# One transformer block on one core: the attention scan takes two keys per step, and GpSimd fills in the products in between and writes the causal mask

## The chip, the core and the metric

The kernel runs on one core of one Trainium2 chip, as one launch. The metric is the device time of that launch in microseconds. The engines that matter here are TensorE (PE in the profile, with its weight loads as PEld), VectorE (DVE), ScalarE (ACT) and GpSimd (POOL); SP is the engine whose queue issues most of the DMAs. Each engine works through its own list of instructions in order, and waits on the others through semaphores.

## The reference

The program is one layer of a block with 1024 tokens, width 1024 and 16 heads of 64. The part that the change touches is stick-breaking attention: no softmax, but a product over the keys between a key and its query.

```python
for i in range(s_len // Q_BLOCK):              # 8 blocks of 128 queries
    n_keys = i * Q_BLOCK + Q_BLOCK             # only the causal prefix of keys
    z = einsum('bhqd,bhkd->bhqk', qb, kp) / sqrt(dh)
    mask = s_idx < t_idx                       # strictly causal
    log_not = where(mask, log_sigmoid(-z), 0.0)
    excl = cumsum(log_not, reverse=True) - log_not
    log_a = log_sigmoid(z) + excl              # A[t,s] = sigmoid(z_ts) * prod_{s<j<t} (1 - sigmoid(z_tj))
    a = where(mask, exp(log_a), 0.0)
    out_i = einsum('bhqk,bhkd->bhqd', a, vp)
```

Around it stand an input projection to eight sections, a short gated convolution as a second branch, two branch projections, a merge by gates, an output projection, and a gated feed-forward layer. All of it is in float32; the kernel splits each float32 matrix into a high and a low part and multiplies them in three passes.

## The kernel before

The kernel works through stages: the start (norm and first projections), the gates and sections with a Strassen scheme, then attention woven together with projections that do not depend on it, then the merge, the output projection and the feed-forward layer. The change lies in the attention stage alone.

There attention is computed as products, not as sums of logarithms. For one head and one block of 128 queries (128 such steps in all, `h` from 0 to 15, `i` from 0 to 7) the tile `pt` of 128 rows of queries by 1024 columns holds 1 - sigmoid(z) for the `(i + 1) * 128` keys of the prefix, at its right end. A running product from the last key to the first turns it into the shares of the stick that are left; the weight of a key is the difference of two neighbouring shares, and that difference is moved onto the values instead (`att_dv`: the tiles `va` and `vb` are the values of neighbouring keys, and their difference is what the weights are multiplied with). So after the scan `pt` goes straight into the product with the values.

A step has these parts, each on its own engine:

- `att_scores`: PE multiplies a block of queries with the keys into `z`, in pieces of at most 512 keys, first the 512 old keys and then the rest (lines 913 and 914, for the high and the low part of the keys). ACT turns each piece into 1 - sigmoid in `pt` (line 915). Blocks 0 to 3 have one piece, blocks 4 to 7 two. `z` has two PSUM buffers.
- `att_scan`: DVE runs the product over all `(i + 1) * 128` columns, from right to left (line 923). Its second operand is `mk`, a constant tile that is 1 where the mask excludes a key and 0 elsewhere; the scan multiplies and then takes the maximum with `mk`, so that excluded keys leave the product at 1.
- `att_trans`: PE transposes `pt` in blocks of 128 columns into PSUM tiles `tr`, four to a tile (line 936). ACT copies a `tr` to the high part `ath` (line 939), DVE subtracts to get the low part `atl` (line 940). `tr` has three buffers.
- `att_av`: for each pair of query blocks PE multiplies the transposed weights with the values (lines 951 and 952) into `o`; ACT and DVE add the last row and put the two halves together (lines 956 and 958), and SP stores the result.

`attention()` is a generator that sets the order: in step `s` come the scores of `s`, the transposes of step `s - 2`, the scan of `s`, and the product with the values of `s - 3`. `pt` has five buffers. After every piece the loop at the end of the stage puts in some of the filler work (`fillers`: two projections with operands that lie ready, lines 1012 to 1014, in groups of three matmuls of 512 columns), in proportion to the attention work done. After that, a loop chains all PE instructions of the stage, and the DVE instructions that attention itself made, in exactly the order in which the program made them; the rest is ordered by the scheduler of the framework. So on PE the distance between the scores of a step and its transposes is fixed: one full step and a bit of filler.

GpSimd has no work in the stage. Its list goes from the weight sums of the gates (line 747) to the first DMA of the stage after attention (line 1127).

Of the kernel before, what the change touches and what calls it, by code (L numbers as in the profile page):

```python
# [12 lines left out]
ALU = mybir.AluOpType  # L13
# [4 lines left out]
P = 128  # L18
T = 1024
D = 1024  # L20
# [10 lines left out]
def block_kernel(tc, x, x_t, cols, ada_1, ada_2, ada_row, w_q, w_kv, w_cg, w_a, w_b, w_o, w_g, w_u, w_d, out):  # L31
    nc = tc.nc
# [7 lines left out]
    def nm(s):  # L40
        uid[0] += 1
        return f"{s}_{uid[0]}"
# [12 lines left out]
    def load_w(src):  # L55
# [32 lines left out]
    mk = const.tile([P, D], F32, name="mk")  # L88
    nc.gpsimd.memset(mk, 0.0)
    nc.gpsimd.affine_select(out=mk[:, D - P:], in_=mk[:, D - P:], compare_op=ALU.is_ge, fill=1.0, base=-1,  # L90
                            pattern=[[-1, P]], channel_multiplier=1)
# [43 lines left out]
    def tt(eng, out, a, b, op):  # L135
        eng.tensor_tensor(out=out, in0=a, in1=b, op=op)  # L136
# [761 lines left out]
    def att_scores(h, i):  # L898

        sqt, skh, skl = hd[h]
        n = (i + 1) * P
        off = D - n
        npt[0] += 1
        pt = pts[npt[0] % NPT]
        ptof[h, i] = pt
        for s0 in range(0, n, 512):  # L910
            m = min(512, n - s0)
            z = pps.tile([P, 512], F32, tag="z", bufs=NZ, name=nm("z"))
            nc.tensor.matmul(z[:, :m], sqt[:, i * P:(i + 1) * P], skh[:, s0:s0 + m], start=True, stop=False)
            lastz[0] = nc.tensor.matmul(z[:, :m], sqt[:, i * P:(i + 1) * P], skl[:, s0:s0 + m], start=False, stop=True)  # L914
            nc.scalar.activation(pt[:, off + s0:off + s0 + m], z[:, :m], AF.Sigmoid, scale=rq[:, 1, i, h:h + 1])  # L915
            if s0 + m < n:
                yield F_Z
        yield F_Z + F_S * ((i - 1) % 8 + 1)

    def att_scan(h, i):  # L920
        pt, off = ptof[h, i], D - (i + 1) * P
        rev = slice(D - 1, off - 1 if off else None, -1)
        nc.vector.tensor_tensor_scan(out=pt[:, rev], data0=pt[:, rev], data1=mk[:, rev], initial=1.0,  # L923
                                     op0=ALU.mult, op1=ALU.max)

    def att_trans(h, i):
        pt, off = ptof.pop((h, i)), D - (i + 1) * P
# [39 lines left out]
    def attention():  # L967

        steps = [(h, i) for h in range(H) for i in (LAST if h == H - 1 else ORDER)]
        for s in range(len(steps) + DAV):  # L970
            flush[0] = s >= len(steps)
            if s < len(steps):
                h, i = steps[s]
                if s % 8 == (0 if h else 3) and h + 1 < H:
                    with tc.issue_after(lastld[0].ins):
                        att_load(h + 1)
                with tc.issue_after(lastz[0].ins) if s else ExitStack():
                    if s in (1, 2):
                        att_dv(0, s - 1)
                    if s % 8 in ((4, 6) if h % 2 else (3, 5)) and h + 1 < H:  # L980
                        att_dv(h + 1, s % 8 // 5)
                    if s % 16 in (6, 7) and s + 16 < len(steps):
                        load_v(2 * (s // 16) + 2, 7 - s % 16)
                if s == 54:
                    with tc.issue_after(lastld[0].ins):
                        vl = load_vlast(1)
                if s == 56:
                    turn_vlast(1, vl)
                yield from att_scores(h, i)
            tr_ = att_trans(*steps[s - 2]) if 0 <= s - 2 < len(steps) else iter(())  # L990
            av_ = att_av(steps[s - DAV][0], steps[s - DAV][1] // 2) if s >= DAV and s % 2 != DAV % 2 else iter(())
            yield from itertools.islice(tr_, 1)
            if s >= DAV and steps[s - DAV][1] == 5:
                yield from av_
            yield from tr_
            if s < len(steps):
                att_scan(*steps[s])
            yield from av_
# [96 lines left out]
    pe, mine = len(nc.cur_bb.bb.instructions), set()  # L1095
# [13 lines left out]
            pass  # L1109
    prev = {}  # L1110
    for i in nc.cur_bb.bb.instructions[pe:]:
        if i.engine == nc.tensor.engine or i.name in mine and i.engine in (nc.vector.engine,):
            if i.engine in prev:
                tc.add_manual_dep(i, prev[i.engine].name, mybir.DependencyInfo(mybir.DependencyClass.NoSync, mybir.DependencyReason.DATA),
                                  reason="in_order")
            prev[i.engine] = i
# [187 lines left out]
    for ch in range(2):  # L1304
# [21 lines left out]
        for i in (0, 4, 1, 2, 3, 5, 6, 7) if ch else range(8):  # L1326
            n, t0 = i // 4, (i % 4) * P
# [114 lines left out]
    def load_any(src):  # L1442
        nld[0] += 1
        if nld[0] % 4 != 1:
            return load_raw(src)
        raw = cp.tile([P, 1024], F32, tag="rawx", bufs=1, name=nm("raw"))
        nc.sync.dma_start(raw, src)
        return raw

    def s2_tile():  # L1450
        return cp.tile([P, 512], F32, tag="s2", bufs=1, name=nm("s2"))

    first = [load_any(w_g[1]), s2_tile(), load_any(w_g[1 + NJ])]
# [309 lines left out]
```

## Time and profile before

| | |
|---|---|
| median of 3 runs | 1811.62 us (1808.80 to 1814.61) |
| the profiled execution | 1812.88 us, of which its span, from the first to the last instruction, is 1811.1 us |
| granted TensorE clock | 0.998 |
| PE busy | 1786.0 us, 99% of the span |
| DVE busy | 1334.5 us, 74% |
| ACT busy | 825.2 us, 46% |
| POOL busy | 202.2 us, 11% |
| scans of attention, line 923 | 128, 172.3 us of DVE in sum, from 598.7 to 969.9 us |

The profile is one execution. Its page gives busy times for each engine, and groups of instructions by source line and tile with their mean duration and the idle time of the engine just ahead of them. A timeline row gives the start and the length in microseconds, the engine, the line, the operation, output and inputs, their shape, and in brackets the idle time of the engine before it with what ended it. Idle time on an engine other than PE costs nothing by itself, since PE is busy nearly all the time; what counts is idle time of PE.

### The profile page before, as it was taken

To read this page: it belongs to the slowest core of one execution; us is meant where nothing else is said; L and a number is where in the kernel's file an instruction comes from. 1 tells how busy PE (TensorE), PEld (TensorE's weight loads), DVE (VectorE), ACT (ScalarE), POOL (GpSimd) and SP (SyncE) were. 2 spreads that over 40 slices of the span, in tenths; PEclk is the share of its full clock that TensorE was granted. 3 is DMA by queue.
4 is the path that set the end of the run, shared out by engine and by line. 5 is a ranking of instruction groups with operands and counts; after the bars stand their busy time and mean duration, and the time that the engine had idled before them with its cause. 6 is when DMAs were issued, how large, how long until landed. Compare 5 with 4: busy or idle time off the path is not lost.

```text
span 1811.1 us, 24342 instructions
## 1 busy us (share of the span) xinstructions
PE 1786.0 (99%) x8599; PEld 1485.4 (82%) x8599; DVE 1334.5 (74%) x2030; ACT 825.2 (46%) x1553; POOL 202.2 (11%) x181
## 2 busy tenths in 40 slices
PE   8999999999999999999999999999999999999999
PEld 6888877888888788888887878888888888878887
DVE  6876586787774799999996764698867777644776
ACT  5534364233433567666675221674544444422321
POOL 0024243723231000000000100100000000000000
PEclk9999999999999999999999999999999999999999
DMA  9479654223545977796645866324533444389876
GB/s 383 162 238 392 231 175 140 87 99 115 211 130 175 266 186 195 214 311 180 159 126 175 278 212 214 129 104 157 217 129 144 147 186 162 130 300 338 279 230 223
DMA packets 165006, 359.04 MB, mean 198 GB/s; under 512 B 15539, under 2 KB 60939, under 8 KB 163733
## 3 DMA queue, kind: packets, MB, share of 16 engines
q1 hardware_dynamic: 128300, 289.65, 48.9%
q10 hardware_dynamic: 33096, 55.25, 8.5%
q0 software_dynamic: 3488, 12.59, 2.1%
q8 instruction: 68, 1.11, 0.3%
q14 instruction: 54, 0.43, 0.1%
HBM read 247.84 MB, written 109.62 MB: 197 GB/s over the span
## 4 chain that ended last, share of the span: by engine, by line
PE 84%; DVE 6%; DMA 6%; ACT 3%; issue 2%; SPq 0%; ACTq 0%; POOL 0%; DVEq 0%
PE pj L293 9%; PE e L133 7%; PE e L131 7%; PE e L132 7%; PE pj L133 7%; PE pj L131 7%; PE pj L132 7%; PE e L1590 4%; PE e L1591 4%; PE e L1592 4%; PE tr L936 3%; PE pj L1012 2%; PE pj L1013 2%; PE pj L1014 2%; PE o L952 2%
## 5 line engine op out<-in xcount | busy, mean ns | idle before, releaser
L923 DVE TENSOR_TENSOR_SCAN pt<-pt,mk 128x128 f32<-128x128 f32 (+7 forms) x128 | 172.3, 1346 | 1.5 <-ACT pt L915 1.5
L1221 ACT ACTIVATE whi<-raw 128x512 fp32r<-128x512 f32 x137 | 84.9, 628 | 159.5 <-PE e L132 100.0
L1222 DVE TENSOR_TENSOR wlo<-raw,whi 128x512 fp32r<-128x512 f32 x137 | 93.0, 686 | 68.3 <-ACT whi L1221 50.7
L293 PE MATMUL pj<-whi,big 128*128 128x512 f32 x448 | 133.8, 396 | 3.5 <-ACT big L262 3.5
L132 PE MATMUL e<-big,whi 128*128 128x512 f32 x352 | 136.9, 389 | 0.0
L133 PE MATMUL e<-big,wlo 128*128 128x512 f32 x352 | 136.3, 389 | 0.5 <-DVE wlo L1222 0.5
L131 PE MATMUL e<-big,whi 128*128 128x512 f32 x352 | 136.5, 390 | 0.0
L136 DVE TENSOR_TENSOR c<-pj,c 128x512 f32<-128x512 f32 x140 | 93.2, 681 | 45.1 <-PE pj L133 44.8
L131 PE MATMUL pj<-big,whi 128*128 128x512 f32 x320 | 125.0, 391 | 0.0
L133 PE MATMUL pj<-big,wlo 128*128 128x512 f32 x320 | 124.8, 390 | 0.0
L132 PE MATMUL pj<-big,whi 128*128 128x512 f32 x320 | 124.6, 389 | 0.0
L1590 PE MATMUL e<-whi,f 128*128 128x512 f32 (+1 forms) x319 | 121.7, 382 | 2.5 <-DMA f<-d_f 2.5
L1591 PE MATMUL e<-wlo,f 128*128 128x512 f32 (+1 forms) x319 | 121.8, 382 | 0.0
L1592 PE MATMUL e<-whi,f 128*128 128x512 f32 (+1 forms) x319 | 121.6, 382 | 0.0
L915 ACT ACTIVATE pt<-z,rq 128x512 f32<-128x512 f32 (+1 forms) x192 | 105.2, 576 | 23.6 <-PE z L914 23.2
L1012 PE MATMUL pj<-big,whi 128*128 128x512 f32 x256 | 113.6, 444 | 0.0
L940 DVE TENSOR_TENSOR atl<-tr,ath 128x512 fp32r<-128x512 f32 (+1 forms) x192 | 102.8, 549 | 9.5 <-ACT ath L939 7.6
L939 ACT ACTIVATE ath<-tr 128x512 fp32r<-128x512 f32 (+1 forms) x192 | 93.0, 488 | 29.2 <-PE tr L936 28.2
L131 PE MATMUL e<-rh,whi 128*128 128x512 f32 x264 | 102.8, 389 | 1.4 <-DVE c L136 1.4
L293 PEld LDWEIGHTS pj<-whi,big 128*128 128x128 f32 x448 | 84.9, 190 | 22.0 <-ACT big L262 4.3
L132 PE MATMUL e<-rl,whi 128*128 128x512 f32 x264 | 102.7, 389 | 0.0
L133 PE MATMUL e<-rh,wlo 128*128 128x512 f32 x264 | 102.0, 389 | 0.0
(298 smaller groups left out, 4571.5 us busy)
## 6 DMA issues: line engine op xcount, KB each, us to landing
f<-d_f SPq DMA_DIRECT2D x77, 512.0 KB, 4.6
d_f<-fs SPq DMA_DIRECT2D x70, 512.0 KB, 3.2
raw<-w_cg SPq DMA_DIRECT2D x40, 512.0 KB, 3.8
raw<-w_u SPq DMA_DIRECT2D x26, 512.0 KB, 4.2
raw<-w_g SPq DMA_DIRECT2D x25, 512.0 KB, 4.1
raw<-w_kv SPq DMA_DIRECT2D x20, 512.0 KB, 5.1
ld<-ada SPq DMA_DIRECT2D x16, 512.0 KB, 6.9
d_t<-ts SPq DMA_DIRECT2D x16, 512.0 KB, 6.6
```

What stands on the lines that cost most here:

```text
L131: nc.tensor.matmul(ps, wh[:, k, :], fh[:, k, :], start=(k == 0 and not onto), stop=False, skip_group_check=onto)
L132: nc.tensor.matmul(ps, wh[:, k, :], fl[:, k, :], start=False, stop=False, skip_group_check=onto)
L133: nc.tensor.matmul(ps, wl[:, k, :], fh[:, k, :], start=False, stop=(k == 3), skip_group_check=onto)
L136: eng.tensor_tensor(out=out, in0=a, in1=b, op=op)
L293: nc.tensor.matmul(ps, a, b, start=(k == 0 and q == 0), stop=(k == KT - 1 and q == 2))
L915: nc.scalar.activation(pt[:, off + s0:off + s0 + m], z[:, :m], AF.Sigmoid, scale=rq[:, 1, i, h:h + 1])
L923: nc.vector.tensor_tensor_scan(out=pt[:, rev], data0=pt[:, rev], data1=mk[:, rev], initial=1.0, op0=ALU.mult, op1=ALU.max)
L940: nc.vector.tensor_tensor(out=tl[:, :nb, c0:c0 + P], in0=src, in1=th[:, :nb, c0:c0 + P].bitcast(F32), op=ALU.subtract)
L1012: nc.tensor.matmul(ps, wh, rh_, start=(k == 0), stop=False)
L1590: nc.tensor.matmul(o, sh, w[0][:, c], start=(j == 0), stop=False)
L1591: nc.tensor.matmul(o, sh, w[1][:, c], start=False, stop=False)
L1592: nc.tensor.matmul(o, sl, w[0][:, c], start=False, stop=(j == NJ - 1))
```

## The change

Three edits, all in attention.

First, the scan takes two keys per step. `first` is every second column of `pt` from the last one down, `both` the columns in between. The scan multiplies its state with an element of `first` and then with the one of `both`, and writes the product into `both`; it has half as many elements and steps by two columns (8 bytes) backwards. The columns of `first` now lack their value: GpSimd multiplies each with the finished product to its right (`mid`, one instruction per step with `(i + 1) * 64 - 1` elements per row, also in steps of 8 bytes). The transposes of a step wait for that product.

Second, the mask. With two multiplications the scan has no place for the maximum, so GpSimd writes 1 into the excluded places of the last 128 columns before the scan (`affine_select`, one per step of 128 by 128). So that these columns are ready early, the pieces of the scores are made in reverse: for blocks 4 to 7 first the piece with the diagonal, of 128 to 512 keys, then the 512 old keys.

Third, the GpSimd instructions that attention makes are chained in the order of the program, as those of DVE are.

```diff
-        for s0 in range(0, n, 512):
+        for s0 in reversed(range(0, n, 512)):
             m = min(512, n - s0)
...
             nc.scalar.activation(pt[:, off + s0:off + s0 + m], z[:, :m], AF.Sigmoid, scale=rq[:, 1, i, h:h + 1])
-            if s0 + m < n:
+            if s0 + m == n:
+                diag = pt[:, D - P:]
+                nc.gpsimd.affine_select(out=diag, in_=diag, compare_op=ALU.is_ge, fill=1.0, base=-1,
+                                        pattern=[[-1, P]], channel_multiplier=1)
+            if s0:
                 yield F_Z
...
     def att_scan(h, i):
         pt, off = ptof[h, i], D - (i + 1) * P
-        rev = slice(D - 1, off - 1 if off else None, -1)
-        nc.vector.tensor_tensor_scan(out=pt[:, rev], data0=pt[:, rev], data1=mk[:, rev], initial=1.0,
-                                     op0=ALU.mult, op1=ALU.max)
+        first = pt[:, slice(D - 1, off, -2)]
+        both = pt[:, slice(D - 2, off - 1 if off else None, -2)]
+        nc.vector.tensor_tensor_scan(out=both, data0=first, data1=both, initial=1.0, op0=ALU.mult, op1=ALU.mult)
+        mid = pt[:, slice(off + 1, D - 2, 2)]
+        tt(nc.gpsimd, mid, mid, pt[:, slice(off + 2, D - 1, 2)], ALU.mult)
...
-        if i.engine == nc.tensor.engine or i.name in mine and i.engine in (nc.vector.engine,):
+        if i.engine == nc.tensor.engine or i.name in mine and i.engine in (nc.vector.engine, nc.gpsimd.engine):
```

The lists of the engines change as follows. On GpSimd, between the weight sums of the gates and the DMAs of the stage after attention, there is nothing before; now 256 rows stand there, two for each step. Before:

```order
L136 TENSOR_TENSOR ws_4977<-raw_4836 128x512
L136 TENSOR_TENSOR ws_4978<-raw_4836,ws_4979 128x512
L747 TENSOR_TENSOR ws_4980<-raw_4834,ws_4978 128x512
L1127 DMA cab_10045<-ada_row 128x1024
L636 DMA ad_10092<-ada 128x1024
```

Now, at the end of the tenth head (blocks 6 and 7) and the start of the eleventh (line 918 is the mask, line 136 the product in between):

```order
L918 AFFINE_SELECT pt_5113<-pt_5113 128x128
L136 TENSOR_TENSOR pt_5113<-pt_5113 128x447
L918 AFFINE_SELECT pt_5109<-pt_5109 128x128
L136 TENSOR_TENSOR pt_5109<-pt_5109 128x511
L918 AFFINE_SELECT pt_5110<-pt_5110 128x128
L136 TENSOR_TENSOR pt_5110<-pt_5110 128x63
```

So the mask of a step stands behind the product of the step before it, which waits for that step's scan. In the same place DVE has these rows before (a scan is printed as SCALAR_TENSOR_TENSOR; `wlo` is the low part of a filler's weights, `mb` a filler's result, `oy` the result of a pair of blocks):

```order
L923 SCALAR_TENSOR_TENSOR pt_5113<-pt_5113,mk 128x896
L958 TENSOR_TENSOR oy_8036<-o_8026,otmp_8035 64x256
L1062 TENSOR_TENSOR mb_8062<-pj_7929,sgi_7927 128x512
L940 TENSOR_TENSOR atl_8008<-tr_8052,ath_8007 128x4x128
L136 TENSOR_TENSOR wlo_8238<-raw_8231,whi_8237 128x512
L940 TENSOR_TENSOR atl_8020<-tr_8065,ath_8019 128x2x128
L923 SCALAR_TENSOR_TENSOR pt_5109<-pt_5109,mk 128x1024
```

and these now:

```order
L928 SCALAR_TENSOR_TENSOR pt_5113<-pt_5113 128x448
L964 TENSOR_TENSOR oy_8352<-o_8342,otmp_8351 64x256
L1068 TENSOR_TENSOR mb_8381<-pj_8232,sgi_8230 128x512
L946 TENSOR_TENSOR atl_8323<-tr_8371,ath_8322 128x4x128
L136 TENSOR_TENSOR wlo_8577<-raw_8570,whi_8576 128x512
L946 TENSOR_TENSOR atl_8335<-tr_8384,ath_8334 128x2x128
L928 SCALAR_TENSOR_TENSOR pt_5109<-pt_5109 128x512
```

The order is the same; each scan has half the elements and no `mk`. On PE only the two pieces of a block's scores change places. Block 5 of one head before:

```order
L913 MATMUL z_6777<-skh_6305,sqt_6304 128x512
L914 MATMUL z_6777<-skl_6306,sqt_6304 128x512
L1012 MATMUL pj_6740<-big_144,whi_6393 128x512
L1013 MATMUL pj_6740<-big_146,whi_6393 128x512
L1014 MATMUL pj_6740<-big_144,wlo_6394 128x512
L913 MATMUL z_6784<-skh_6305,sqt_6304 128x256
L914 MATMUL z_6784<-skl_6306,sqt_6304 128x256
L936 MATMUL tr_6788<-dm,pt_5113 128x128 x4
```

and now:

```order
L913 MATMUL z_6957<-skh_6433,sqt_6432 128x256
L914 MATMUL z_6957<-skl_6434,sqt_6432 128x256
L1018 MATMUL pj_6915<-big_144,whi_6528 128x512
L1019 MATMUL pj_6915<-big_146,whi_6528 128x512
L1020 MATMUL pj_6915<-big_144,wlo_6529 128x512
L913 MATMUL z_6967<-skh_6433,sqt_6432 128x512
L914 MATMUL z_6967<-skl_6434,sqt_6432 128x512
L942 MATMUL tr_6971<-dm,pt_5113 128x128 x4
```

The PE list has the same rows otherwise, and the lists of ACT and SP differ from before only by rows that changed places with a neighbour or two.

## The prediction

> **What bounds the kernel now.** I read the page's busy times first, then the busy times of the attention stage (600 to 985 us), then who makes PE wait there.
>
> ```profile
> PE 1786.0 (99%) x8599; PEld 1485.4 (82%) x8599; DVE 1334.5 (74%) x2030; ACT 825.2 (46%) x1553; POOL 202.2 (11%) x181
> 600.00:985.00 385.00, 377.71 (x2309) 325.66 (x2307) 353.69 (x497) 256.64 (x581) 2.35 (x4) 1.00 0.72 200
> PE tr L936 <- DVE pt L923: 4.3, 9, 1.8
> PE o L951 <- ACT ath L939: 1.1, 1, 1.1
> PE o L952 <- DVE atl L940: 0.7, 3, 0.3
> PE tr L936 <- DVE atl L940: 0.4, 1, 0.4
> PE z L913 <- ACT pt L915: 0.3, 1, 0.3
> ```
>
> The second row is the stage: its length, then the busy time of PE, PEld, DVE, ACT, POOL. PE is the bound of the kernel and of the stage: 377.71 of 385 us. DVE comes close, 353.69 us or 92%, and has to answer in its fixed order. POOL is empty. The whole prize is what PE idles here: 385 - 377.71 = 7.3 us of 1811. The wait rows (total, times, longest) say that the scan is the main cause, nine times.
>
> The idle column understates a wait. Ends of matmuls are modelled, so starts are the better measure:
>
> ```profile
> 828.46 0.28 PE L914 MATMUL z<-skl,sqt 128*128 128x128 f32 x1
> 828.57 0.63 PE L936 MATMUL tr<-dm,pt 128*128 128x128 f32 x4
> 832.28 0.28 PE L914 MATMUL z<-skl,sqt 128*128 128x256 f32 x1
> 832.77 0.63 PE L936 MATMUL tr<-dm,pt 128*128 128x128 f32 x4 [0.21 <-DVE pt L923]
> ```
>
> Undisturbed, the transposes start 0.11 us behind the last score matmul; with the wait it is 0.49. The row calls it 0.21, PE lost 0.38. So I add 0.17 us to each wait.
>
> Two waits are not DVE's fault and stay. The longest one on the scan is at the start of the stage, where DVE itself waits for a DMA:
>
> ```profile
> 601.83 0.69 DVE L136 TENSOR_TENSOR vb<-vb,va 128x512 f32<-128x512 f32 x1 [2.60 <-DMA vb<-d_v]
> 602.44 0.68 DVE L923 TENSOR_TENSOR_SCAN pt<-pt,mk 128x256 f32<-128x256 f32 x1
> 603.18 0.44 PE L936 MATMUL tr<-dm,pt 128*128 128x128 f32 x2 [1.80 <-DVE pt L923]
> ACT whi L516 <- DMA raw<-w_cg: 3.1, 1, 3.1
> ```
>
> The other is the 1.1 us on `ath`: ACT had stood 3.1 us before a filler weight's DMA. **Removable** is then 7.3 - 1.8 - 1.1 = 4.4 us, plus 0.17 for each of the 13 other waits of the list, 2.2 us: 6.6 us.
>
> **The change part by part.** *The scan* loses half its elements, 128 times.
>
> ```profile
> L923 DVE TENSOR_TENSOR_SCAN pt<-pt,mk 128x128 f32<-128x128 f32 (+7 forms) x128 | 172.3, 1346 | 1.5 <-ACT pt L915 1.5
> L923 DVE TENSOR_TENSOR_SCAN pt<-pt,mk 128x1024 f32<-128x1024 f32 x16 | 36.5, 2279 | 0.0
> L923 DVE TENSOR_TENSOR_SCAN pt<-pt,mk 128x128 f32<-128x128 f32 x16 | 6.6, 414 | 1.5 <-ACT pt L915 1.5
> ```
>
> Between 128 and 1024 elements a scan costs (2279 - 414) / 896 = 2.08 ns per element, on a fixed 0.148 us. With 64 to 512 elements a head's eight scans take 8 x 0.148 + 2304 x 2.08 ns = 5.98 us, all 16 heads 95.6 us, so DVE gains 76.7 us. No row shows a scan in steps of 8 bytes. The bounds are this price and, with a step of two at half the speed, the old 172.3 us. I take the first: the scan already runs backwards at 2 ns per element, so one element has time for two words.
>
> *The product in between*, and *the mask*, are new on POOL. Rows for POOL:
>
> ```profile
> L136 POOL TENSOR_TENSOR ws<-raw,raw 128x512 f32<-128x512 f32 x20 | 29.0, 1452 | 222.1 <-DMA raw<-w_cg 130.5 <-DMA raw<-w_q 29.9 <-DVE cab L136 17.9
> L123 POOL TENSOR_TENSOR rs_r<-rs_m,nhalf 128x8 f32<-128x8 f32 x16 | 28.8, 1800 | 1.2
> L123 POOL TENSOR_TENSOR rs_r<-rs_m,nhalf 128x1 f32<-128x1 f32 x8 | 4.4, 556 | 0.7
> L90 POOL TENSOR_SCALAR_AFFINE_SELECT mk<-mk 128x128 f32<-128x128 f32 x1 | 0.3, 290 | 0.0
> ```
>
> The mask is the same instruction as on line 90: 128 x 0.29 = 37 us. The two small rows are powers, whose elements are dear (1800 - 556) / 7 = 178 ns, but they give the fixed part: 556 - 178 = 0.378 us. The 512-element row then gives (1452 - 378) / 512 = 2.10 ns per element. A head's products have 63 to 511 elements, 2296 in sum: 8 x 0.378 + 2296 x 2.10 ns = 7.85 us, all heads 126 us. POOL is then busy 163 of the stage's 385 us. These rows are contiguous; for steps of 8 bytes the bounds are 2.10 and 4.2 ns (half speed). I take 2.10, the row it is nearest to.
>
> [...]
>
> *The new chain.* A step's transposes now wait for sigmoid, mask, scan and product, and the next step's mask stands behind that product, so steps form a loop over two engines. A handover between them is short: POOL starts 0.09 us behind DVE in the first pair of rows, DVE 0.03 us behind POOL in the second.
>
> ```profile
> 150.10 0.67 DVE L454 TENSOR_REDUCE qss<-qsq 128x8 f32<-128x512 f32 x1
> 150.86 0.20 POOL L122 TENSOR_SCALAR rs_m<-qss 128x8 f32<-128x8 f32 x1 [4.94 <-DVE qss L454]
> 161.91 1.64 POOL L123 TENSOR_TENSOR rs_r<-rs_m,nhalf 128x8 f32<-128x8 f32 x1
> 163.58 0.69 DVE L457 TENSOR_TENSOR qn<-pj,rs_r 128x512 f32<-128x512 f32 x1 [0.79 <-POOL rs_r L123]
> L923 DVE TENSOR_TENSOR_SCAN pt<-pt,mk x128: 411/1346/2281, 598.7 to 969.9; 128x128 f32<-128x128 f32 x16, 128x256 f32<-128x256 f32 x16, 128x384 f32<-128x384 f32 x16, 128x512 f32<-128x512 f32 x16
> ```
>
> Per head the loop is 5.98 + 7.85 + 2.32 + 24 x 0.1 = 18.6 us, while a head has (969.9 - 598.7) / 16 = 23.2 us. It does not bind on average. The tight place is a head's end, where short steps follow the longest scan. I replay it at 828 us:
>
> ```profile
> 825.71 2.01 DVE L923 TENSOR_TENSOR_SCAN pt<-pt,mk 128x896 f32<-128x896 f32 x1
> 828.00 0.38 ACT L939 ACTIVATE ath<-tr 128x256 fp32r<-128x256 f32 x1
> 829.42 0.68 DVE L136 TENSOR_TENSOR wlo<-raw,whi 128x512 fp32r<-128x512 f32 x1
> 830.01 0.42 DVE L940 TENSOR_TENSOR atl<-tr,ath 128x256 fp32r<-128x256 f32 x1
> 830.35 2.28 DVE L923 TENSOR_TENSOR_SCAN pt<-pt,mk 128x1024 f32<-128x1024 f32 x1
> ```
>
> Before, the long scan starts at 830.35, behind DVE's backlog, and ends past 832.6; PE wanted it at 832.28 + 0.11 = 832.39. Now the scan of block 6 takes 1.08 us instead of 2.01, so the rows behind it come about 0.9 us sooner (the copy at 828.00 feeds the last of them early enough): the long scan starts at 829.4, takes 1.21 and ends at 830.6, and the product of 0.378 + 511 x 2.10 ns = 1.45 us, with a handover, ends at 832.15. PE finds it 0.25 us ahead of need. The mask ahead of that scan is no hindrance: the product of block 6 ends near 828.2, the mask near 828.5. So this wait goes, with a thin margin; earlier blocks are shorter, with the same two steps of cover.
>
> What is worse: after the late `vb` the scan takes 0.41 instead of 0.68 us, but a product of 0.65 and a handover follow, so PE starts about 0.5 us later, once. Queued behind a scan that now waits for its mask are DVE's next subtractions for `atl`, and the filler's; DVE's load falls to 353.7 - 76.7 = 277 of 385 us, which covers that. The swapped pieces put the 512-key sigmoid last, a few tenths of a us later for the scan, inside the two steps. No DMA is added; PE's matmuls are the same.
>
> [...] In the gates' stage POOL and DVE work at once.
>
> ```profile
> 240.00:560.00 320.00, 320.00 (x1415) 261.81 (x1414) 233.83 (x339) 124.77 (x208) 124.99 (x84) 1.00 0.39 134
> L136 DVE TENSOR_TENSOR wlo<-ws,whi 128x512 fp32r<-128x512 f32 x65 | 51.3, 799 | 20.6 <-ACT whi L516 20.5
> L136 DVE TENSOR_TENSOR c<-pj,c 128x512 f32<-128x512 f32 x115 | 76.6, 681 | 27.4 <-PE pj L133 27.3
> L136 DVE TENSOR_TENSOR wlo<-raw,whi 128x512 fp32r<-128x512 f32 x30 | 20.3, 680 | 2.2 <-ACT whi L516 2.2
> ```
>
> With POOL busy 125 of 320 us (39%) the DVE operation with both inputs in SBUF takes 799 ns; the last row is its like in attention, without POOL, at 680. The one that reads PSUM stays at 681. So 119 ns per two-input operation at 39%; at POOL's 42% in attention, for some 90 of them beside the scans, 12 us of DVE, against 76.7 gained. The scan has two SBUF inputs too, but by the order of the lists no POOL instruction can run during it: the product before it is over, its own comes after. I charge 0.2 us on PE for a product that is held up.
>
> [...]
>
> **Sum:** 6.6 removed, 0.5 and 0.2 added: 5.9 us less. The profiled execution's span goes from 1811.1 to 1805.2 us; its own time, 1812.88, is 1.3 above the median, so against the median of 1811.62 I predict **1805.7 us**.
>
> **The rivals.** *The wait moves to POOL and nothing is won* (18%). If a product's element costs 1.5 times the row, 3.15 ns, the product at a head's end takes 1.99 us, 0.54 more than the 1.45 above; 0.25 of it is covered, so each of 16 heads waits 0.29 + 0.17 us, 7.4 us on top of the sum: 1805.7 + 7.4 = 1813.
>
> *The gain is lost at the stage's end* (10%). There PE waits for ACT, which stands before a load of `yr`:
>
> ```profile
> 976.87 8.10 DMA yr<-d_ya
> 984.99 0.64 ACT ya L1164
> ```
>
> If that load does not come sooner, half of the gain is given back: about 1808.7. Against it: the load starts behind DVE work of the same stretch, which shifts too.
>
> *POOL becomes the bound: slower* (13%). At steps of 8 bytes and 4.2 ns per element the loop of a head becomes 18.6 + 4.8 = 23.4 us, more than its 23.2; DVE's other work still has to fit in. At a head's end the product comes 1.07 us later, 0.25 of it covered, plus 0.17, and in the step before 0.94 later, perhaps half of it felt: about 1.4 us per head, 23 us for all. On top of the sum: 1805.7 + 23 = 1829. It decides from about 1.5 times the row on, where the rival above stands. The POOL rows are all contiguous, so nothing in the trace excludes it.
>
> *The scan does not get shorter* (7%). If a step of two halves its speed, a head's loop is 10.8 + 7.85 + 2.32 + 2.4 = 23.4 us and DVE is as full as before; the long scan ends at 832.6 as now, the product comes 1.55 us behind it: about 1.8 us per head more and nothing removed: 1811.6 + 29 = 1841.
>
> **How the numbers follow.** The forecast gets 52%; its own range is 1803.5 to 1808.5, from all of the removable with nothing added to half of it. A change can be told from none here at about 0.3%, 5.4 us, so 1806.2 is the border and lies inside the forecast: 0.36 of its 0.52 are faster, 0.16 same. The moved wait gives 0.02 faster, 0.14 same, 0.02 slower; the stage's end 0.04 and 0.06. Sum: faster 0.42, same 0.36, slower 0.22. The range is 1803 to 1818: below nothing is left to remove (7.3 plus hidden starts, 8.6 us at the most), above it takes in the moved wait up to some 1.75 times the row and leaves out the two rivals with 20%.
>
> **What would show it.** Right: scans of 512 elements near 1.21 us, products of 511 elements near 1.45 us, masks near 0.3 us, DVE busy near 290 us between 600 and 985, PE waiting on `pt` only near 603 us. Wrong: products near 2.5 us, or a row in which PE's transposes wait for POOL many times; a scan of 512 still at 2.2 us; or PE idle behind `yr` longer than 1.4 us.

## The result, and the profile after

The changed kernel takes 1804.02 us (median of 6 runs, 1801.86 to 1806.53), the kernel before in the same comparison 1811.88. The ratio is 0.9953 with a 95% interval of [0.9938, 0.9968]: 8.5 us faster, 5.8 to 11.2. Repeated later beside other kernels (`a1_again`, below), the same kernel came to 0.9954 [0.9942, 0.9966]. The prediction was 1805.7 us, 5.9 less than before: right in direction and place, and some 2.5 us too careful.

The profiled execution took 1806.53 us, with a span of 1804.5 us and a granted clock of 0.997. Its page has these busy times:

```profile
PE 1785.0 (99%) x8599; PEld 1486.4 (82%) x8599; DVE 1271.7 (70%) x2030; ACT 829.8 (46%) x1553; POOL 343.0 (19%) x437
```

The view of windows has the attention stage (length, then PE, PEld, DVE, ACT and POOL, each with its count, the granted clock, the DMA share and GB/s):

```profile
600.00:985.00 385.00, 381.40 (x2342) 331.15 (x2341) 296.00 (x507) 265.76 (x590) 144.28 (x259) 1.00 0.73 206
```

And the view of waits says who made PE wait between 600 and 985 us (total, times, longest):

```profile
PE tr L942 <- POOL pt L136: 2.4, 2, 1.9
PE o L957 <- ACT ath L945: 1.1, 1, 1.1
```

In the 385 us from 600 DVE is busy 296.0 instead of 353.69, POOL 144.28 instead of 2.35, and PE idles 3.6 instead of 7.3 us. Nine waits of PE on the scan have become two waits on the product, both in the first steps of the stage. The list of waits on `atl` is gone.

The stage itself, from the first score matmul to the last product with the values (start of both, from PE's rows), went from 390.4 to 382.2 us, 8.2 less; everything outside it takes 1420.7 and 1422.3 us. So the whole gain lies in the stage. The 1.6 us more outside it are about what one stretch at a granted clock of 0.50 costs, 3.41 us from 1589.55 us on, behind a wait of PE for a load that before has too, without that stretch.

The parts, grouped by line and shape, for DVE and then for POOL (busy time, mean ns of one, idle time before):

```profile
L928 DVE TENSOR_TENSOR_SCAN pt<-pt 128x512 f32<-128x512 f32 x16 | 19.4, 1215 | 0.0
L136 DVE TENSOR_TENSOR wlo<-raw,whi 128x512 fp32r<-128x512 f32 x31 | 26.6, 861 | 3.4 <-ACT whi L516 3.3
```

```profile
L918 POOL TENSOR_SCALAR_AFFINE_SELECT pt<-pt 128x128 f32<-128x128 f32 x128 | 45.7, 357 | 48.7 <-ACT pt L915 48.6
L136 POOL TENSOR_TENSOR pt<-pt 128x511 f32<-128x511 f32 x16 | 17.6, 1099 | 44.9 <-DVE pt L928 42.8 <-ACT ath L945 2.0
L136 POOL TENSOR_TENSOR pt<-pt 128x319 f32<-128x319 f32 x16 | 18.9, 1183 | 21.9 <-DVE pt L928 13.9 <-ACT pt L915 6.4 <-ACT ybh L1039 1.5
L136 POOL TENSOR_TENSOR pt<-pt 128x63 f32<-128x63 f32 x16 | 4.7, 295 | 25.2 <-DVE pt L928 25.2
```

The scan of 512 elements takes 1215 ns where 1.21 us was forecast, and the kernel before needs 1214 ns for 512 elements in steps of 4 bytes: the step of 8 bytes is free. The product of 511 elements takes 1.10 us where 1.45 was forecast, the mask 0.357 where 0.29 was.

### The profile page after: what moved, and what is told of

It reads as the page before. It is cut to its first block, busy times and chain, and to the rows that moved or that the text cites. A ratio compares the mean times of both kernels' runs of the same rounds, so it can differ in the third digit from the quotient of the medians.

```text
span 1804.5 us, 24915 instructions
## 1 busy us (share of the span) xinstructions
PE 1785.0 (99%) x8599; PEld 1486.4 (82%) x8599; DVE 1271.7 (70%) x2030; ACT 829.8 (46%) x1553; POOL 343.0 (19%) x437
## 4 chain that ended last, share of the span: by engine, by line
PE 88%; DMA 4%; DVE 3%; ACT 2%; issue 1%; POOL 1%; ACTq 0%; SPq 0%; DVEq 0%; POOLq 0%
PE pj L293 9%; PE e L133 7%; PE e L131 7%; PE e L132 7%; PE pj L133 6%; PE pj L131 6%; PE pj L132 6%; PE pj L1018 4%; PE pj L1020 4%; PE pj L1019 4%; PE e L1596 4%; PE e L1598 4%; PE e L1597 4%; PE tr L942 3%; PE o L958 2%; PE z L913 2%
## 5 line engine op out<-in xcount | busy, mean ns | idle before, releaser
L136 POOL TENSOR_TENSOR pt<-pt 128x63 f32<-128x63 f32 (+7 forms) x128 | 101.8, 795 | 212.0 <-DVE pt L928 195.7
L1228 DVE TENSOR_TENSOR wlo<-raw,whi 128x512 fp32r<-128x512 f32 x137 | 93.2, 687 | 67.3 <-ACT whi L1227 49.8
L915 ACT ACTIVATE pt<-z,rq 128x128 f32<-128x128 f32 (+1 forms) x192 | 107.3, 579 | 26.7 <-PE z L914 23.7
L136 DVE TENSOR_TENSOR wlo<-raw,whi 128x512 fp32r<-128x512 f32 x108 | 88.6, 824 | 29.8 <-ACT whi L516 29.6
```

## The experiments

Three things were open. Is the gain really DVE's relief, or one of the small edits that came with it? Does it matter that the product is on GpSimd? And how much dearer may the product be before the chain over two engines decides?

**Give DVE its time back.** This is the changed kernel with a reduction behind each scan, as long as the part of the scan that was saved; nobody reads the result.

```diff
         nc.vector.tensor_tensor_scan(out=both, data0=first, data1=both, initial=1.0, op0=ALU.mult, op1=ALU.mult)
+        if i:
+            nc.vector.tensor_reduce(out=one, in_=mk[:, :128 * i], op=ALU.add, axis=AX.X)
```

> The changed kernel, with a reduction of 128*i columns of a constant put behind each scan on DVE (one input in SBUF, result unused), so that DVE has about as much to do as before: some 75 us more in the attention stage. Theory (the gain is DVE's relief): PE's waits come back, and the GpSimd product stands behind a late scan, so the time is that of before or worse, 1811 to 1820 us. Rival (the gain comes from the order of the pieces, or from the mask being out of the scan): the time stays near 1804.

Measured: 1813.53 us, ratio 1.0010 [1.0001, 1.0019]. The whole gain is gone. The stage of this kernel in the view of windows, and then PE's waits:

```profile
600.00:985.00 385.00, 379.11 (x2312) 325.35 (x2310) 351.93 (x612) 259.71 (x582) 142.50 (x258) 1.00 0.72 201
```

```profile
PE tr L944 <- POOL pt L136: 4.5, 10, 1.0
```

DVE is back at 351.93 us, and PE waits ten times for 4.5 us, before the product now, because the scan ahead of it is late. What the change won depends on DVE's time.

**The small edits alone.** The kernel before with only the reversed pieces of the scores (`e5_swap`), and the kernel before with the reversed pieces, the mask by GpSimd and the chained GpSimd order, but with the full scan (`e6_mask`). The four lines of the mask below belong to `e6_mask` alone, whose line for the GpSimd order is left out here.

```diff
-        for s0 in range(0, n, 512):
+        for s0 in reversed(range(0, n, 512)):
...
-            if s0 + m < n:
+            if s0 + m == n:
+                diag = pt[:, D - P:]
+                nc.gpsimd.affine_select(out=diag, in_=diag, compare_op=ALU.is_ge, fill=1.0, base=-1,
+                                        pattern=[[-1, P]], channel_multiplier=1)
+            if s0:
```

> The kernel before with the pieces of the scores in reverse order alone. Theory: nothing or a little loss, 1811 to 1813, since the scan then waits for the 512-key sigmoid. Rival (part of the gain is the order of the pieces): 1807 to 1809.

> The kernel before with the reversed pieces, the mask written by GpSimd and the GpSimd order, but the old full scan with its own mask operand: everything of the change but the halved scan and the product. Theory (the gain is DVE's relief): no gain, 1811 to 1814, a little slower since each scan also waits for the mask. Rival (mask or order bring the gain): 1806 to 1808.

Measured: 1813.63 us, ratio 1.0003 [0.9995, 1.0012], and 1813.03 us, ratio 1.0007 [0.9997, 1.0016]. Neither gains anything. With the mask moved and the scan as long as before, PE still waits nine times for the scan (a row of the waits of `e6_mask`):

```profile
PE tr L940 <- DVE pt L927: 3.9, 9, 1.0
```

**The product on DVE instead.** The mask stays on GpSimd, the product goes back to the engine that the change wanted to relieve.

```diff
-        tt(nc.gpsimd, mid, mid, pt[:, slice(off + 2, D - 1, 2)], ALU.mult)
+        tt(nc.vector, mid, mid, pt[:, slice(off + 2, D - 1, 2)], ALU.mult)
```

> The changed kernel with the product in between on DVE instead of GpSimd; the mask stays on GpSimd. [...] Theory (DVE's load sets the waits): between the two kernels, 1805 to 1809. Rival (only the move to GpSimd brings the gain, halving the scan does not): 1811 or more.

Measured: 1804.3 us, ratio 0.9958 [0.9944, 0.9971], not to be told from the change and just below the range that was expected. Its stage in the view of windows, and two of DVE's groups:

```profile
600.00:985.00 385.00, 380.93 (x2330) 329.77 (x2329) 340.62 (x628) 260.57 (x584) 57.42 (x131) 1.00 0.73 204
```

```profile
L136 DVE TENSOR_TENSOR pt<-pt 128x511 f32<-128x511 f32 x16 | 11.1, 696 | 0.4
L136 DVE TENSOR_TENSOR wlo<-raw,whi 128x512 fp32r<-128x512 f32 x30 | 20.5, 683 | 1.6 <-ACT whi L516 1.6
```

DVE makes the 511 products in 696 ns, against GpSimd's 1099, and without a handover. It stays busy 340.62 us, only 13 less than before, and that is enough, where the 1.8 us less of `e1_pad` were not: the relief needed was small. And without products on GpSimd, `wlo` is back at 683 ns.

**Leave the product out.** Every second weight then keeps its plain value; GpSimd makes only the mask.

```diff
-        tt(nc.gpsimd, mid, mid, pt[:, slice(off + 2, D - 1, 2)], ALU.mult)
```

> The changed kernel without the product in between on GpSimd (the odd columns then keep their plain values, so the attention weights of half the keys are not computed); transposes wait for the scan alone. Theory (the product is hidden but for the first steps): 1803 to 1804, PE's wait near 603 us shorter by about 0.5 us. Rival (the product costs PE a good part of what DVE's relief brings): 1801 or less.

Measured: 1806.96 us, ratio 0.9973 [0.9964, 0.9982]. Work was taken away, and the kernel is not faster than the change; its median is some 3 us higher, though the two intervals overlap a little. The profile says where. In the row of PE below, its product with the values waits 4.09 us near the end of the stage; the view of windows has the stretch behind that wait (the last three columns are the granted clock, the DMA share and GB/s):

```profile
979.48 0.58 PE L956 MATMUL o<-ath,vt 128*128 128x256 f32 x1 [4.09 <-ACT ath L944]
979.40:984.20 4.80, 4.72 (x16) 4.15 (x17) 2.51 (x5) 3.97 (x6) 0.00 (x0) 0.50 0.58 191
```

After the pause PE runs for 4.8 us at a granted clock of 0.50. The pause is that of the prediction's second rival, only longer: ACT stands before a load of `yr`, and its copy to `ath` stands behind that. Here are two of these loads as they are issued and as ACT reads them, and a load of GpSimd's own list, `cab`, in this kernel:

```profile
960.12 0.77 POOL L1132 DMA_DIRECT2D cab<-ada_row  x1 [0.99 <-PE tr L941]
960.68 0.32 SPq L1165 DMA_DIRECT2D yr<-d_ya  x1
966.07 0.63 ACT L1169 ACTIVATE ya<-yr 128x512 fp32r<-128x512 f32 x1 [4.44 <-DMA yr<-d_ya]
969.50 0.40 SPq L1165 DMA_DIRECT2D yr<-d_ya  x1
978.31 0.63 ACT L1169 ACTIVATE ya<-yr 128x512 fp32r<-128x512 f32 x1 [6.56 <-DMA yr<-d_ya]
```

and in the changed kernel:

```profile
962.05 0.32 SPq L1166 DMA_DIRECT2D yr<-d_ya  x1
965.07 0.63 ACT L1170 ACTIVATE ya<-yr 128x512 fp32r<-128x512 f32 x1 [2.07 <-DMA yr<-d_ya]
965.88 0.77 POOL L1133 DMA_DIRECT2D cab<-ada_row  x1
968.54 0.42 SPq L1166 DMA_DIRECT2D yr<-d_ya  x1
976.61 0.63 ACT L1170 ACTIVATE ya<-yr 128x512 fp32r<-128x512 f32 x1 [3.88 <-DMA yr<-d_ya]
```

SP issues 16 loads of `yr` and ACT reads 16, in the same order; shown are the eighth and the eleventh. PE's pause hangs on the eleventh. Without the product it is issued 5.9 us before PE wants `ath` (969.50 against 979.48 - 4.09), in the change 8.2 us before. The rows lead further back. The load `cab` stands in GpSimd's list behind the last product; without products GpSimd comes to it sooner, just ahead of the eighth load of `yr`, and that one then takes 5.4 us to ACT's reading instead of 3.0. `yr` has two buffers, so the later loads wait for this reading.

One profile can be chance, so the same kernel ran again.

> The kernel without the product once more, as in its first run (every second weight keeps its plain value, so the result differs). Its first profile had one PE wait of 4.1 us behind ACT, which stood before a load of yr, and PE's matmuls ran at half their pace for some 4 us after it. Theory that this was a chance of DMA timing: this profile has less than 2 us there, the granted clock after it stays at 1.00, and the ratio is 0.994 to 0.996. Rival: without the product the queue of SP always comes to the loads of yr at a bad time: 3 us or more of PE idle there again, and a ratio near 0.997.

Measured: 1807.12 us, ratio 0.9979 [0.9967, 0.9992], the same once more. The profiled execution is the fastest of the ten, and still has the pause and, in the view of windows, the half clock:

```profile
PE o L956 <- ACT ath L944: 2.2, 1, 2.2
```

```profile
976.40:979.50 3.10, 3.04 (x10) 2.65 (x11) 2.04 (x4) 2.83 (x4) 0.00 (x0) 0.50 0.88 326
```

Neither expectation fits as it was written: the wait of 2.2 us lies between the two, and the loss in the median is the rival's. The order of the loads is the same again: `cab` is issued at 958.96, the eighth `yr` at 959.54 and read 5.1 us later, and the eleventh goes out 6.1 us before PE wants `ath`. So the extra wait is no accident of one execution, and it eats what the lighter GpSimd might have won. In all 14 profiles of this study the eighth load takes 3.6 to 5.4 us to its reading where `cab` goes out ahead of it (the eight without products on GpSimd), and 2.9 to 3.1 us where `cab` goes out behind it (the six with them, `e1_pad` and its full DVE among them). So the product on GpSimd seems to do something that nobody planned: it holds back a load until a better time. This is read from the rows; no run moved `cab` alone.

**The product twice.** The change with the product made twice (each weight in between is multiplied by its neighbour twice). It prices the rival in which POOL becomes the bound.

```diff
         tt(nc.gpsimd, mid, mid, pt[:, slice(off + 2, D - 1, 2)], ALU.mult)
+        tt(nc.gpsimd, mid, mid, pt[:, slice(off + 2, D - 1, 2)], ALU.mult)
```

> The changed kernel with the product in between done twice in a row on GpSimd (the odd columns get the factor twice, so their weights are not those of the reference): the long product takes about 2.2 us instead of 1.1, and the mask of the next step comes later too. Theory (the cover at a head's end is some 0.25 us plus what the product turned out cheaper, 0.35): each head waits 0.5 + 0.17 us, 11 us in all, 1815. Rival (there is ample cover): 1804 to 1806.

Measured: 1834.26 us, ratio 1.0126 [1.0112, 1.0140], 30 us more than the change and far more than expected. The stage in the view of windows, PE's waits, and the view of the scan's line:

```profile
600.00:985.00 385.00, 360.20 (x2181) 305.30 (x2181) 284.93 (x477) 250.25 (x558) 226.44 (x372) 1.00 0.69 189
```

```profile
PE tr L943 <- POOL pt L136: 24.3, 27, 2.4
```

```profile
L928 DVE TENSOR_TENSOR_SCAN pt<-pt x128: 278/754/1225, 600.0 to 994.5; 128x64 f32<-128x64 f32 x16, 128x128 f32<-128x128 f32 x16, 128x192 f32<-128x192 f32 x16, 128x256 f32<-128x256 f32 x16
```

GpSimd is busy only 59% of the stage, and yet it is the bound. The loop of the prediction goes part of the way: scan, product, mask, scan, in turn on two engines. Per head it is 6.0 us of scans, 12.3 of products, 2.8 of masks and (the prediction's estimate) 2.4 of handovers, 23.5 us, where the change has a head every (963.5 - 600.0) / 16 = 22.7. The measured head is (994.5 - 600.0) / 16 = 24.7 us, so the sum has 0.8 of the 2.0 us that were added; the rest was not taken apart. That the loop binds shows on DVE as well: its scans wait 65 times, 45.7 us in all, for the mask, where the change has 12 waits and 3.7 us. Neither engine is full; the chain over both decides.

**The start of the stage.** The wait that the prediction left alone stands where DVE's list has the subtraction on `vb` ahead of the second scan, and `vb` arrives late. Moving that subtraction one step later takes the scan out from behind the load:

```diff
-                    if s in (1, 2):
-                        att_dv(0, s - 1)
+                    if s in (2, 3):
+                        att_dv(0, s - 2)
```

It ran on the change (`e7_late`), on the kernel before (`e8_before_late`), and beside the change itself (`a1_again`), all three on the same chip.

> The changed kernel once more, to stand beside the next two on the same chip: 1804 us.

> The changed kernel with the first head's two value operations (the difference of the two value tiles, and its split) one step later, so that DVE does not stand before the value load ahead of the second scan. Theory (the 1.9 us wait of PE near 604 us is that load, not GpSimd): about 2 us less than the changed kernel, 1802, and no wait of PE at that place. Rival (the wait only moves to the next step): 1804.

> The kernel before with the same move alone. Theory (this wait has nothing to do with the change): about 2 us less than before, 1810. Rival (DVE is so full there that the later operations delay the next scans as much): 1811 to 1812.

Measured: 1804.76 us, ratio 0.9954 [0.9942, 0.9966]; 1802.22 us, 0.9943 [0.9931, 0.9955]; 1812.13 us, 1.0000 [0.9990, 1.0010]. So the move brings nothing to the kernel before and some 2.5 us by the medians to the change, though the two intervals overlap. The 2 us that the theory of `e8_before_late` expected did not come. In its profile the longest wait on the scan is 0.9 instead of 1.8 us, but PE's waits on `ath` at 666 and 987 us grew from 1.1 and 1.4 to 1.3 and 1.9 us, and behind each came 3.41 us at a granted clock of 0.50; that is one execution. PE's waits on the product in `a1_again` and then in `e7_late` show both what is won and where it goes:

```profile
PE tr L942 <- POOL pt L136: 3.7, 1, 3.7
```

```profile
PE tr L942 <- POOL pt L136: 1.7, 2, 1.4
```

In `a1_again` the late load cost PE 3.7 us instead of the 1.9 of the first profile, since the load's landing differs between executions, and the granted clock was 0.50 from 604.84 to 607.94 us behind it. With the move 0.25 us are left at that place, and 1.4 at the next step, whose scan now stands behind the same load. `e7_late` is the fastest kernel of the study.

**Both at once.** The product on DVE, and the later subtraction.

> The product on DVE and the first product with the values one step later, both at once. If the gain is DVE's relief alone, and the later step takes only the wait at the start, the two add up to no more than the later step alone: 1801.5 to 1803.5 us, ratio 0.9935 to 0.995. If the chain over GpSimd costs something that the later step hides, this one is faster still, below 1801. If DVE at 340 of 385 us is too full for it, 1804 to 1806, with PE waiting for DVE several times between 600 and 985 us.

Measured: 1806.26 us, ratio 0.9977 [0.9965, 0.9989]. The edits do not add up; the result lies just past the third expectation, DVE too full. Its stage and PE's waits:

```profile
600.00:985.00 385.00, 381.13 (x2335) 329.67 (x2335) 341.36 (x629) 262.76 (x585) 57.25 (x131) 1.00 0.72 205
```

```profile
PE tr L942 <- DVE pt L136: 2.2, 4, 0.9
PE o L958 <- DVE atl L946: 0.6, 2, 0.4
```

PE waits for DVE six times again. Against `e7_late`, whose only difference is the engine of the product, the intervals do not meet (the two ran on different chips, each against the kernel before on its own). So with the start of the stage mended GpSimd is the better place for the product; in the change as it stands it is worth no more than can be measured. That a full DVE is the whole reason is not shown: here, too, `cab` goes out ahead of the eighth load of `yr` (961.04 and 961.92), which takes 4.5 us, in `e7_late` behind it (964.86 and 961.04) with 3.0 us.

**What a product costs by itself.** The changed kernel with 42 products on the idle constant tile at the kernel's start, six of each size and step, in this order: 511 elements in steps of 4 and of 8 bytes, 255 in steps of 4, 8 and 16, 340 in steps of 4 and of 12.

> The changed kernel with GpSimd products on a constant tile put into the feed-forward stage, six each of: 511 elements contiguous and in steps of 2; 255 contiguous, in steps of 2 and of 4; 340 contiguous and in steps of 3 (4, 8, 12 and 16 bytes). Only their durations are read, the shortest of each six, since DVE operations can hold them up. Theory (a step of 8 bytes is free on GpSimd): steps of 2 cost what contiguous costs, 1.1 us for 511. Rival (the price grows with the step): steps of 2 dearer by a tenth or more. [...]

In the trace they do not run in the feed-forward stage: nothing holds them back, and they stand at the start. Measured: 1816.04 us, since they hold up the first projections (they ran between 7.9 and 64.4 us); the durations are what counts. Three of POOL's rows:

```profile
7.86 1.04 POOL L136 TENSOR_TENSOR mk<-mk 128x511 f32<-128x511 f32 x1 [5.45 <-DMA d_v<-mk]
16.09 1.37 POOL L136 TENSOR_TENSOR mk<-mk 128x511 f32<-128x511 f32 x1
17.54 1.37 POOL L136 TENSOR_TENSOR mk<-mk 128x511 f32<-128x511 f32 x1
```

The first row is the first product, in steps of 4 bytes: 1.04 us, and 1042 ns is also the mean of the 511 elements in steps of 8 in `e1_pad`. The second and third are the last in steps of 4 and the first in steps of 8, in a stretch where DVE is busy 8.06 of 8.10 us: 1.37 both. Of 340 elements, the last product in steps of 4 and the first in steps of 12, both with DVE idle, take 0.75 and 0.78 us; of 255 elements beside the same DVE operations, steps of 4, 8 and 16 take 938, 940 and 976 ns. So 8 bytes cost nothing and 12 or 16 some 4%. The place in the list counts for more: the 511 elements take 1.04 to 1.97 us, by the author's estimate because of the DVE operation that runs beside them, as the rows of 319 elements in the change suggest (last section).

## Why the prediction came out as it did

**The mechanism was right.** DVE's lateness was the cause of most of the waits (`e1_pad`, `e5_swap`, `e6_mask`), and a shorter scan removes them. The rivals fall: the scan did get shorter; behind POOL's products PE loses time only at the start, and three times 0.2 to 0.3 us by its starts; POOL is not the bound, though it would be with twice the products.

**The replay of a head's end held, by two errors that cancel, which is luck.** The forecast was that the product is done 0.25 us before PE needs it. The same place in the changed kernel, DVE, POOL and PE (a row of scores, then the transposes):

```profile
826.32 1.22 DVE L928 TENSOR_TENSOR_SCAN pt<-pt 128x512 f32<-128x512 f32 x1
827.68 1.04 POOL L136 TENSOR_TENSOR pt<-pt 128x511 f32<-128x511 f32 x1 [3.39 <-DVE pt L928]
828.77 0.28 PE L914 MATMUL z<-skl,sqt 128*128 128x256 f32 x1
828.89 0.60 PE L942 MATMUL tr<-dm,pt 128*128 128x128 f32 x4
```

PE wants it at 828.77 + 0.11 = 828.88 and has it at 827.68 + 1.04 = 828.72, 0.16 ahead. Counted back from that score matmul, the scan starts 2.45 us ahead where 2.88 was forecast, 0.43 late; the product is 0.41 us shorter than forecast.

**The sum, term by term.** How much longer PE's starts lie apart than those of the same pair usually do (the lower quartile of each kind), before and after, from PE's rows in the trace, where the forecast has its term:

| place | before | after | change | forecast |
|---|---|---|---|---|
| start of the stage, behind `vb` (two steps) | 2.3 | 2.7 | +0.4 | +0.5 |
| the 13 waits that were to go | 7.1 | 0.7 | -6.4 | -6.6, and +0.2 for a product held up |
| the wait on `ath` at 665 us, behind `raw` | 1.2 | 0 | -1.2 | 0 |
| the end of the stage, behind `yr` | 1.5 | 1.2 | -0.3 | 0 |
| all gaps together | 36.7 | 28.6 | -8.1 | -5.9 |

The large term, with its 0.17 us for what the idle column hides, came out within 0.2 us. The 0.2 us for a product held up was the author's estimate, and no run shows it as such: in the change eight products of 319 elements took 1.49 to 2.10 us instead of 0.72, and what PE lost by its starts behind the later products is the three times 0.2 to 0.3 us. Its 7.3 us of idle time hold some 0.5 that no row of the waits names and that were counted as removable without a reason. Of the 2.2 us that are missing, 1.2 lie in one place. **The step that failed** is the sentence that the wait of 1.1 us on `ath` at 665 us is "not DVE's fault and stays". It went away. The rows of before:

```profile
656.95 0.68 DVE L136 TENSOR_TENSOR vt<-vb,vt 128x512 fp32r<-128x512 f32 x1
657.66 0.48 SPq L844 DMA_DIRECT2D vb<-d_v  x1
660.58 0.48 SPq L505 DMA_DIRECT2D raw<-w_cg  x1
664.99 0.63 ACT L516 ACTIVATE whi<-raw 128x512 fp32r<-128x512 f32 x1 [3.14 <-DMA raw<-w_cg]
666.74 0.39 PE L951 MATMUL o<-ath,vt 128*128 128x256 f32 x1 [1.05 <-ACT ath L939]
```

and of after:

```profile
655.70 0.68 DVE L136 TENSOR_TENSOR vt<-vb,vt 128x512 fp32r<-128x512 f32 x1
656.41 0.53 SPq L844 DMA_DIRECT2D vb<-d_v  x1
658.50 0.82 SPq L505 DMA_DIRECT2D raw<-w_cg  x1
663.02 0.63 ACT L516 ACTIVATE whi<-raw 128x512 fp32r<-128x512 f32 x1 [1.08 <-DMA raw<-w_cg]
```

SP's load of the next `vb` is issued 0.03 us after DVE's subtraction on the old one ends, in both. The filler's weights stand behind that load in SP's queue, and ACT behind the weights (4.4 and 4.5 us from issue to ACT). DVE's 1.25 us sooner, and 0.8 less between the two loads in SP's queue (not followed further), bring the weights 2.1 us sooner, and PE no longer waits. The prediction ended its way back at the DMA and did not ask what that DMA's queue stood behind. Across the runs ACT stands 3.1 to 3.4 us at this place in the four kernels with the full scan, and 0.6 to 1.3 in the change, its repeat, `e7_late`, `e3_prod_dve` and `e10_late_dve`; `e1_pad` has 1.5 and `e2_again` 1.2, both without a wait on `ath`, `e2_noprod` 2.6 with a short one. So this is read from the rows and agrees with most runs, but no run moved that one load alone. The wait may also be worth more than its length: in `e5_swap` and `e8_before_late` 3.41 us at a granted clock of 0.50 follow it, which the profile of before happens not to have. The prediction's sum has no term for that, and what it adds to the median was not measured.

The range ended at 1803 because nothing was thought to be left below: 8.6 us at the most. `e7_late`, at 1802.22, shows that there was.

**Prices that were off and did not matter.** The product: 0.378 us and 2.10 ns per element were taken from powers and contiguous sums; from its own rows it is (1099 - 295) / 448 = 1.79 ns on about 0.18 us, 102 us in sum instead of 126. Part of that is DVE's doing: in `e1_pad`, where DVE runs the added reduction, of one input, behind each scan, the same rows of 63 and 511 elements take 293 and 1042 ns, 1.67 ns per element. The mask: 0.357 instead of 0.29 us. DVE's operations beside GpSimd's work: `wlo` rose from 680 to 861 ns, 181 more where 119 were taken from the gates' stage. None of them reached PE: a head's end kept its 0.16 us, and DVE has 89 us of the stage to spare (385 less 296.0).

**The rival of a POOL bound** was priced near what it costs, though it did not come: it put a loop of 23.4 us per head at 23 us of time, and with the product made twice a loop of 23.5 us cost 30. Its threshold, 1.5 times the row's price per element, or 8 x 0.378 + 2296 x 3.15 ns = 10.3 us of products per head, lies between the 6.4 us of the change and the 12.3 us here. The expectation of `e4_prod_twice` was far lower than the prediction's own arithmetic, and was wrong. **The rival at the stage's end** did not come either, the wait behind `yr` stayed near a microsecond; but its mechanism is what stopped `e2_noprod`.

## What to carry to other kernels

When the bounding engine waits a little on a second engine that is nearly full, a small cut of the second one's work can be worth all of those waits, and more need not be worth anything: 13 us less of DVE brought as much as 58. Follow a wait that ends at a DMA further back, to what the queue that issued it stood behind, before calling it independent of the change. Before taking work off an idle engine, look at what stands behind that work in its list: a load may now go out at a worse time. And when work is split over two engines that hand over to each other, add up the loop: at 59% and 74% busy the two set the pace together.

## What the runs showed of the hardware that was not expected

- **A pause of PE was followed by half the clock in some places and not in others, and its length alone does not tell which.** In `e2_again` a wait of 2.2 us was followed by 3.1 us at a granted clock of 0.50, in `e2_noprod` one of 4.1 us by 4.8 us, in `e8_before_late` already one of 1.3 us; in before a wait of 2.5 us, which ends at 1597.19 us, was not. These rows are two neighbouring stretches of 3.41 us in `e8_before_late`, and two in before (length, PE's busy time first; the granted clock third from the end):

```profile
664.30:667.71 3.41, 1.75 (x10) 1.08 (x9) 2.02 (x4) 3.05 (x7) 0.00 (x0) 1.00 1.08 284
667.71:671.12 3.41, 3.41 (x16) 3.12 (x15) 3.41 (x4) 1.08 (x4) 0.00 (x0) 0.50 1.17 221
1592.72:1596.13 3.41, 1.96 (x9) 1.29 (x7) 3.41 (x7) 2.84 (x6) 0.00 (x0) 1.00 0.80 243
1596.13:1599.54 3.41, 2.35 (x10) 1.99 (x11) 3.41 (x7) 0.00 (x0) 0.42 (x1) 1.00 0.95 341
```

  PE is busy for 1.75 of the 3.41 us ahead of the fall in `e8_before_late`, and for 1.08 of those ahead of the one in the change (1586.14 to 1589.55 us). The two stretches in before have 1.96 and 2.35 us; but of the 3.41 us up to the end of its wait (1593.78 to 1597.19 us) PE is busy for only 0.90, and the clock stays at 1.00. So the busy share just ahead does not tell it either; what does was not shown, and no run was made to test it.
- **DVE operations and products on GpSimd took longer where they met; with masks alone this hardly shows.** On the mean `wlo` takes 680 ns in before, 683 in `e3_prod_dve` and 682 in `e2_noprod` with masks alone, and 861 in the change. Single rows say more: in the change the one at 619.90 us, which meets a product of 511 elements, takes 1.53 us, the one at 621.96 us, which meets nothing on GpSimd, 0.68. The reverse was seen as well: of the 16 products of 319 elements in the change, the eight that meet DVE's `vt<-vb,vt`, which reads two SBUF tiles, take 1.49 to 2.10 us, and the eight that do not take 0.72 to 0.73, which makes their mean of 1183 ns larger than that of 511 elements.
- **The step of the product's operands cost nothing at 8 bytes and little at 12.** In `e9_step` 511 elements take 1.37 us in steps of 4 and of 8 bytes; 340 elements take 0.75 us in steps of 4 and 0.78 in steps of 12, 4% more.
